# The modulation vector's groups on VectorE: spread over heads two to eight

## The chip, the core and the metric

The kernel runs on one core of a Trainium2 chip. The core has a matrix engine (TensorE), three engines for elementwise work (VectorE, ScalarE, GpSimd), and SyncE, whose queue issues the DMAs. The metric is the device time of one execution in microseconds, as the median of several runs. All engines run side by side and wait for each other on semaphores.

## The reference, cut to what matters

One inference step of a one-layer backbone on 2048 latent tokens and 128 context tokens, with 1024 channels:

```
mod   = split(silu(c) @ ada_w + ada_b, 6)      # for latents, and the same with c_ctx for context
h     = rms_norm(x, norm_mix_w) * (1 + mod[1]) + mod[0]
y     = hgrn2_mixer(h)                         # 8 heads: projections, two scans in chunks, gate, w_out
x     = x + mod[2] * y
h     = rms_norm(x, norm_ffn_w) * (1 + mod[4]) + mod[3]
x     = x + mod[5] * conv_ffn(h)
y_out = rms_norm(x, final_norm_w)
```

The modulation vector `mod` has 6 x 1024 numbers for the latents and as many for the context. The kernel holds it as 48 columns of 128 numbers, eight columns for each of the six parts. Parts 0 and 1 are needed before the first head. Parts 2 to 5, columns 16 to 47, are needed only after the eight heads: part 2 when the mixer's output is added to the residual, the others in the feed-forward part.

## The kernel before, in words

**Stages.** The tokens are cut into pieces of 512 (four of latents) and one of 128 (context). After a start that computes the first columns of `mod` and the first norm, a loop goes over the eight heads. For each head and each piece it projects the normed tokens to a query, two forget gates, a value and an output gate (matmuls of lines 416 to 418 and 538 to 540), and runs the chunkwise scan. Then comes the output projection (`project`, line 950), the second norm, and the feed-forward part in two stages (lines 1076 and 1307), which together take up more than the second half of the time.

**The scan's steps.** A head has eight steps, two for each latent piece; the context piece's projections come in the eighth. The scan of a head is cut into small units, and `scan_steps` (line 803) says into which step each goes, so that a unit runs while TensorE is at the projections of later pieces. The units of a head reach nine steps beyond its own eight, into the next head, and for head eight into the output projection. Three of them matter here. `unit1a` (line 577) is VectorE's work on decays, some forty instructions. `unit2` (line 673) multiplies keys and values on TensorE (line 692), copies a part on ScalarE (line 698) and updates the forward state on VectorE (lines 708 and 710). `unit3` (line 713) forms the output on TensorE and reads that state (line 730). So line 730 waits for line 708, and that for line 692.

**The groups.** Columns 16 to 47 are computed without TensorE. `ada_one(j)` (line 319) loads 128 rows of transposed weights (512 KB) through SyncE's queue into a buffer of the tag `wr`, and VectorE multiplies them by the broadcast conditioning vector and sums along the row, once for the latents and once for the context:

```
nc.sync.dma_start(raw, adaT[i * P : (i + 1) * P, :])
for s in range(2):
    junk = rt([P, D], F16, "og" if tag == "wr" else "SB")
    V.scalar_tensor_tensor(junk, raw, 1.0, cs[s], ALU.mult, ALU.mult,
                           accum_out=mod[:, j, s : s + 1])
```

These two instructions are called a group here, and one of them a half. There are 32 groups, and the loop over heads calls one at the end of each step from the second head on (lines 910 to 912) until column 48 is reached: with eight steps in a head that is heads two to five. Behind the loop, small VectorE instructions add the bias (`ada_add`, line 282) and form the factors `wmod` (line 332) and `g64` (line 917). The two broadcast vectors `cs`, 4 KB in each partition each, are kept until the last group.

**Other loads.** `load_w` (line 405) loads the weights of the next head in the eighth step, in buffers of the same tag `wr`, and splits them on ScalarE and VectorE (line 413); behind the loop it does so with the output weights (`load_wo`, line 945).

**What sets the order.** The text of the program sets the order only in part. The tile framework puts the instructions of each engine in an order of its own, by the program's order as priority and by when it holds their inputs to be ready; each engine then takes its queue strictly in that order. SyncE's queue, with all DMA issues, is such a queue too. The places of the buffers in on-chip memory are planned by the kernel itself (`place`, line 109): it runs the program once with stand-ins that note at which operation each buffer is born and last used, and lays them out so that addresses are reused late.

Of the kernel before, what the change touches and what calls it, by code (L numbers as in the profile page):

```python
# [170 lines left out]
def backbone_kernel(ctx: ExitStack, tc: tile.TileContext, **io):  # L171
# [16 lines left out]
    def no_probe(shape, *_):  # L188
        return Probe(0, 0)

    stages(Counts(clock), probe, no_probe, no_probe, **io)
    for t in keep:
        t.last = NEVER
# [15 lines left out]
    def drt(shape, dt, tag):  # L209
        return dr.tile(shape, dt, tag=tag, name=tag)  # L210

    stages(nc, tl, pt, drt, **io)


def stages(nc, tl, pt, drt, xT, adaH, adaT, pvec, w_in, w_out, w_up, w_down, state, yT, st_out):
# [103 lines left out]
    def ada_one(j, tag="wr"):  # L319

        raw = rt([P, D], F32, tag)
        i = j - 4 if j < 8 else j - 12
# [5 lines that stand above are left out]
# [52 lines left out]
    def tick():  # L380

        for g in list(norms):
            if next(g, 0) == 0:
                norms.remove(g)
# [39 lines left out]
    def load_x(p):  # L424
        t0, n = PIECES[p]
        XS[p] = []
        if p == CTX:
            xc = rt([P, KT, n], F32, "wr")
            get = lambda k: xc[:, k]
        else:  # L430
            get = eight(("even", "odd", "lv", "lv")[p], [P, 512], F32)
        for k in range(KT):
            x = get(k)
            nc.sync.dma_start(x[:, :n], xT[k * P : (k + 1) * P, t0 : t0 + n])
            XS[p].append(x)
# [16 lines left out]
    def norm1(p, eng):  # L452
        begin(norm(XS[p], PIECES[p][1], SQ3, "o16", eng, lambda bc: norm1_out(p, bc)))
# [33 lines left out]
    def head_weights(hd):  # L487
        for i in range(3):
            head_qf(hd, i)
        head_vg(hd)  # L490
# [24 lines left out]
    def project_qf(hd, p, i):  # L515

        pj = pt([P, 512], "pj")
        qf_mm(hd, p, i, pj, range(KT))
        qf_out(hd, p, i, pj)

    def project_vg(hd, p):

        n = PIECES[p][1]
        nb = n // P
        hp = H[p]
        small = n != 512
        wvg = WT[hd][1]
        st = PC[hd, p]
        vt = tl([P, n], F32, "vc") if small else rt([P, 512], F32, "v")
        sg = tl([P, n], F32, "sgc") if small else rt([P, 512], F32, "sg")  # L530
        for j0 in range(0, nb, 2):
            m = min(2, nb - j0)
            pj = pt([P, 2, 2, P], "pj")
            for jj in range(m):
                tok = slice((j0 + jj) * P, (j0 + jj + 1) * P)
                o = pj[:, :, jj, :]
                for k in range(KT):
                    T.matmul(o, hp[k][:, 0, tok], wvg[0][:, k], start=(k == 0), stop=False)  # L538
                    T.matmul(o, hp[k][:, 0, tok], wvg[1][:, k], start=False, stop=False)  # L539
                    T.matmul(o, hp[k][:, 1, tok], wvg[0][:, k], start=False, stop=(k == KT - 1))  # L540
            A.activation(vt[:, j0 * P : (j0 + m) * P].rearrange("p (b c) -> p b c", c=P),
                         pj[:, 0, :m], AF.Copy, scale=IWS)
            A.activation(sg[:, j0 * P : (j0 + m) * P].rearrange("p (b c) -> p b c", c=P),
                         pj[:, 1, :m], AF.Silu, scale=IWS)
        st["v"] = vt
        st["sg"] = sg
# [293 lines left out]
    def run(items):  # L840
        for f, *args in items:
            f(*args)
# [39 lines left out]
    nada = [16]  # L882

    for hd in range(HEADS):
        for p in range(CTX):
            for part in range(2):
                i = hd * NSEG + 2 * p + part
                run(before[i])
                if i < 2:
                    tick()  # L890
                else:
                    project_qf(hd, p, 2 * part)
                    tick()
                run(mid.get(i, []))
                if part == 1:
                    project_vg(hd, p)
                elif i > 0:
                    project_qf(hd, p, 1)
                if (p, part) == (3, 1):
                    for i3 in range(3):  # L900
                        project_qf(hd, CTX, i3)
                    project_vg(hd, CTX)
                    if hd + 1 < HEADS:
                        head_weights(hd + 1)
                run(after[i])
                if i in (1, 3, 5):
                    if i == 3:
                        load_x(3)
                    norm1((i + 3) // 2, V)
                if hd > 0 and nada[0] < 48:  # L910
                    ada_one(nada[0])
                    nada[0] += 1
    ada_add(16, 48, mod[:, 16:48])
# [562 lines left out]
```

## Time and profile before

| | |
|---|---|
| median of 3 runs | 2772.4 us (2771.98 to 2774.57) |
| the profiled execution | 2777.14 us, its span 2775.2 us |
| TensorE matmul / weight loads busy | 2705.4 / 2129.1 us |
| VectorE busy | 1886.0 us |
| ScalarE busy | 1071.8 us |
| DMA, mean rate | 86 GB/s |
| the 64 instructions of the groups | 182.6 us (first start) to 758.3 us (last start) |

The span runs from the first to the last instruction of the profiled execution. Busy time is the time in which an engine has at least one instruction of compute under way. Line numbers (L326) are those of the kernel, and tile names are those of the program. A group's row gives busy time and mean duration, then the idle time of the engine ahead of it and what ended it. A row of a timeline begins with start and duration in microseconds; a wait stands in brackets with the instruction that ended it. A row of stretches begins with the stretch and its length, then for each engine the busy time and, in brackets, the number of instructions; at the end stand the granted TensorE clock as a share of full speed, the DMA share and the rate.

The heads in this profile, from the start of a head's first projection: head two at 179.8 us, three at 325.7, four at 470.2, five at 614.1, six at 757.9, seven at 901.8, eight at 1045.6; head eight's projections end at 1190.2 us.

### The profile page before, as it was taken

Reading aid. Unit: us, or ns where it says so; the run is one execution under the profiler, and the core shown is the slowest. Engines: PE = TensorE matmul, PEld = TensorE weight load, DVE = VectorE, ACT = ScalarE, POOL = GpSimd, SP = SyncE. Lnnn points to the kernel's source line nnn. Section 1 sums busy time; section 2 is a strip of 40 time slices with the busy share of each in tenths; the row PEclk is TensorE's granted clock in tenths of the full one; section 3 lists DMA queues with packets and bytes.
Section 4 is the critical chain, followed back from the end, with each engine's and each line's share of the span. In section 5 each row is a group of like instructions: output and inputs, shape, how many; then the busy total and the mean of one; then the engine's idle time right before and its main releaser. Section 6 shows DMA issues by size and latency. Waiting matters only on the chain.

```text
span 2775.2 us, 57195 instructions
## 1 busy us (share of the span) xinstructions
PE 2705.4 (97%) x23576; PEld 2129.1 (77%) x23576; DVE 1886.0 (68%) x5324; ACT 1071.8 (39%) x2373; POOL 72.9 (3%) x84
## 2 busy tenths in 40 slices
PE   8999999999999999999999999999999999999998
PEld 4677777777777677765578888888888988888887
DVE  7887887887876766755996767666677677623123
ACT  5533334343434242513664545445455453300000
POOL 0100000000000000000000000000000000000000
PEclk9999999999999999999999999999999999999999
DMA  7011213121201010345112232221212275344352
GB/s 265 27 63 42 70 34 95 32 74 39 73 6 54 6 54 4 110 137 194 67 41 85 63 89 67 73 86 56 86 58 77 77 200 170 127 156 137 123 166 73
DMA packets 194005, 239.73 MB, mean 86 GB/s; under 512 B 12368, under 2 KB 148432, under 8 KB 193744
## 3 DMA queue, kind: packets, MB, share of 16 engines
q1 hardware_dynamic: 193744, 236.08, 26.9%
q8 instruction: 185, 3.03, 0.5%
q14 instruction: 76, 0.62, 0.1%
HBM read 166.44 MB, written 69.60 MB: 85 GB/s over the span
## 4 chain that ended last, share of the span: by engine, by line
PE 58%; DVE 16%; DMA 5%; ACT 2%; issue 2%; POOL 0%; SPq 0%; DVEq 0%; POOLq 0%; ACTq 0%
PE pj_p L1307 11%; PE pj_p L1076 9%; PE sc_p L1076 6%; PE pj_p L418 5%; PE pj_p L416 5%; PE pj_p L417 5%; DMA r<-w_up 3%; PE pj_p L539 3%; PE pj_p L538 3%; PE pj_p L540 3%; DMA ud<-u 2%; DVE u L971 2%; PE sc_p L1307 1%; PE sc_p L692 1%; DVE wd L1233 1%
## 5 line engine op out<-in xcount | busy, mean ns | idle before, releaser
L1076 PEld LDWEIGHTS <-w 128*128 128x128 f16 x7392 | 725.0, 98 | 115.4 <-issue 29.7
L1076 PE MATMUL pj_p<-T,w 128*128 128x256 f16 x4224 | 491.0, 274 | 24.2 <-DVE c L1082 16.4
L1307 PEld LDWEIGHTS <-wd 128*128 128x128 f16 x3696 | 361.5, 98 | 53.5 <-issue 8.8
L1076 PE MATMUL sc_p<-T,w 128*128 128x256 f16 x3168 | 367.8, 273 | 0.0
L1307 PE MATMUL pj_p<-U,wd 128*128 128x256 f16 x3168 | 354.3, 273 | 5.7 <-DVE x L1316 5.7
L416 PE MATMUL pj_p<-H,wp 128*128 128x512 f16 x768 | 291.2, 380 | 2.8 <-ACT H L395 2.4
L417 PE MATMUL pj_p<-H,wp 128*128 128x512 f16 x768 | 292.6, 381 | 0.5 <-DVE H L400 0.4
L418 PE MATMUL pj_p<-H,wp 128*128 128x512 f16 x768 | 292.3, 381 | 0.0
L540 PE MATMUL pj_p<-wp,H 128*128 128x256 f16 x1024 | 279.1, 273 | 0.0
L538 PE MATMUL pj_p<-wp,H 128*128 128x256 f16 x1024 | 279.1, 273 | 0.0
L539 PE MATMUL pj_p<-wp,H 128*128 128x256 f16 x1024 | 279.1, 273 | 0.0
L1316 DVE SCALAR_TENSOR_TENSOR x<-pj_p,g,x 128x256 f32<-128x256 f32 x96 | 46.4, 483 | 211.6 <-PE pj_p L1307 211.5
L418 PEld LDWEIGHTS <-wp 128*128 128x128 f16 x960 | 94.2, 98 | 91.4 <-issue 2.6
L416 PEld LDWEIGHTS <-wp 128*128 128x128 f16 x960 | 94.3, 98 | 83.5 <-issue 4.2
L417 PEld LDWEIGHTS <-wp 128*128 128x128 f16 x960 | 94.2, 98 | 81.1 <-issue 2.0
L363 ACT ACTIVATE n<-x 128x256 f32<-128x256 f32 (+1 forms) x63 | 25.0, 403 | 262.9 <-DVE x L1316 201.9
L1103 ACT ACTIVATE y<-c,pv,cws 128x512 f32<-128x512 f32 x88 | 71.2, 811 | 137.1 <-DVE c L1082 133.9
L511 ACT ACTIVATE f<-pj_p 128x512 f32<-128x512 f32 x64 | 38.0, 596 | 185.2 <-PE pj_p L418 185.1
L539 PEld LDWEIGHTS <-H 128*128 128x128 f16 x1024 | 100.2, 98 | 11.8
L540 PEld LDWEIGHTS <-H 128*128 128x128 f16 x1024 | 100.2, 98 | 11.7
L538 PEld LDWEIGHTS <-H 128*128 128x128 f16 x1024 | 100.3, 98 | 11.5
L417 PE MATMUL pj_p<-og,wo 128*128 128x512 f16 (+1 forms) x320 | 108.9, 349 | 0.0
(281 smaller groups left out, 5037.6 us busy)
## 6 DMA issues: line engine op xcount, KB each, us to landing
ud<-u SPq DMA_DIRECT2D x44, 896.0 KB, 4.8
U<-ud SPq DMA_DIRECT2D x56, 704.0 KB, 4.9
r<-w_up SPq DMA_DIRECT2D x44, 512.0 KB, 4.0
wr<-w_in SPq DMA_DIRECT2D x40, 512.0 KB, 4.2
wr<-adaT SPq DMA_DIRECT2D x32, 512.0 KB, 3.7
rawd<-w_down SPq DMA_DIRECT2D x20, 704.0 KB, 8.1
x<-xT SPq DMA_DIRECT2D x32, 256.0 KB, 5.3
sp<-oT SPq DMA_DIRECT2D x32, 256.0 KB, 2.2
```

The source lines that it names most:

```text
L416: T.matmul(out, whl[0], hhl[:, 0, :n], start=first, stop=False)
L417: T.matmul(out, whl[0], hhl[:, 1, :n], start=False, stop=False)
L418: T.matmul(out, whl[1], hhl[:, 0, :n], start=False, stop=last)
L511: A.activation(ft, pj[:, :n], AF.Tanh, scale=0.5 * IWS)
L538: T.matmul(o, hp[k][:, 0, tok], wvg[0][:, k], start=(k == 0), stop=False)
L539: T.matmul(o, hp[k][:, 0, tok], wvg[1][:, k], start=False, stop=False)
L540: T.matmul(o, hp[k][:, 1, tok], wvg[0][:, k], start=False, stop=(k == KT - 1))
L971: V.tensor_tensor(dst[1], src, dst[0], ALU.subtract)
L1076: T.matmul(out, wt[:, a, ks], tt[:, b, k], start=first and k == 0 and n == 0, stop=i in (2, 3, 4) and k == 3 and n == 2, skip_group_check= ...
L1103: A.activation(y, a, AF.Identity, bias=pv[:, PV_CB + cb : PV_CB + cb + 1], scale=cws[:, 22 + cb : 23 + cb])
L1307: T.matmul(out, w[:, a, k], UT[p, zb][b][:, k], start=first and i % 2 == 0 and k == 0 and q == 0, stop=n in (2, 3, 4) and k == KP - 1 and ...
L1316: V.scalar_tensor_tensor(x, get(src), g64[:, 1, m, 0:1], x, ALU.mult, ALU.add)
```

## The change

One condition is added. A group is now called only in steps whose number `i` (counted through all heads, eight to a head, from 0) gives `4 * i % 7` below 4, that is in four of every seven steps:

```diff
-                if hd > 0 and nada[0] < 48:
+                if hd > 0 and nada[0] < 48 and 4 * i % 7 < 4:
                     ada_one(nada[0])
                     nada[0] += 1
     ada_add(16, 48, mod[:, 16:48])
```

`i` runs from 8 to 63 in heads two to eight; 32 of these 56 numbers fulfil the condition, so all 32 groups are still called inside the loop, the last one in step 63, the eighth of head eight. The instructions of a group, its load and its tags are the same as before. With the calls, the births and last uses of the buffers move, those of `cs` among them, and so the plan of the places is drawn anew.

## The prediction

> **What bounds the kernel now.** I read the page first, for which engine fills the span, and then went to the part that the change touches: the scan over heads two to eight.
>
> ```profile
> span 2775.2 us, 57195 instructions
> ...
> PE 2705.4 (97%) x23576; PEld 2129.1 (77%) x23576; DVE 1886.0 (68%) x5324; ACT 1071.8 (39%) x2373; POOL 72.9 (3%) x84
> ```
>
> TensorE is busy for 97% of the span, VectorE for 68%. The average mixes stages, so the second view is the busy time by head. I cut the span where TensorE begins the projections of a head; heads two to five hold all 32 groups, heads six to eight none.
>
> ```profile
> core 0: us, PE busy (x) PEld busy (x) DVE busy (x) ACT busy (x) POOL busy (x), PEclk, DMA share, GB/s
> ...
> 179.80:325.70 145.90, 144.04 (x1206) 103.95 (x1204) 116.16 (x443) 51.77 (x136) 5.33 (x5) 1.00 0.18 53
> 325.70:470.20 144.50, 143.97 (x1208) 104.05 (x1206) 117.16 (x454) 51.83 (x137) 5.24 (x5) 1.00 0.19 58
> 470.20:614.10 143.90, 143.90 (x1208) 103.92 (x1206) 119.02 (x458) 52.37 (x137) 4.83 (x5) 1.00 0.18 58
> 614.10:757.90 143.80, 143.80 (x1207) 104.02 (x1206) 116.92 (x448) 52.14 (x137) 4.79 (x5) 1.00 0.19 58
> 757.90:901.80 143.90, 143.90 (x1208) 103.94 (x1206) 103.82 (x446) 52.14 (x137) 5.09 (x5) 1.00 0.10 29
> 901.80:1045.60 143.80, 143.80 (x1207) 103.97 (x1206) 99.99 (x426) 52.05 (x137) 5.36 (x5) 1.00 0.09 29
> 1045.60:1190.20 144.60, 144.19 (x1210) 104.20 (x1208) 106.30 (x437) 55.88 (x141) 4.71 (x5) 1.00 0.22 66
> ```
>
> This table carries most of the argument. The first number after each stretch is its length. Heads four and five carry the groups and take 143.9 and 143.8 us; heads six and seven carry none and take 143.9 and 143.8 us. VectorE is busy for 119.0 and 116.9 us in the first pair and for 103.8 and 100.0 us in the second, and the length doesn't notice: TensorE has no gap in any of the four. Only heads two (145.9), three (144.5) and eight (144.6) are longer, by 2.1, 0.7 and 0.8 us over 143.8.
>
> The third view says what TensorE waited for from head two until just behind head eight. Its columns are the total, the number of times and the longest.
>
> ```profile
> PE sc_p L730 <- DVE SF L708: 4.4, 2, 3.1
> PE sc_p L661 <- ACT oT L769: 1.1, 2, 0.6
> PE sc_p L692 <- ACT kT L670: 0.4, 1, 0.4
> ```
>
> Over 1,023 us that is 5.9 us of waiting, of which VectorE causes 4.4 us in two waits, both at the same place: the output matmul of line 730 wants the forward state that line 708 writes. So the whole prize within these heads is small, and the question is what the change does to these two waits.
>
> **The change part by part.** The groups themselves are moved, not removed.
>
> ```profile
> L326 DVE SCALAR_TENSOR_TENSOR og<-wr,wp 128x1024 f16<-128x1024 f32 x64 | 76.3, 1217 | 1.7 <-DMA wr<-adaT 1.6
> ```
>
> The 64 instructions take 76.3 us, so a group of two takes 2.4 us and one of its halves 1.2 us. By the new rule (step number times four, modulo seven, below four) heads two to eight get 4, 5, 4, 5, 4, 5 and 5 groups, 32 in all, the last in the last step of head eight. VectorE thus loses 4, 3, 4 and 3 groups in heads two to five (9.5 or 7.2 us each) and gains 4, 5 and 5 in heads six to eight (9.5, 11.9, 11.9 us). As heads four to seven show, neither matters to the length of a head that is filled by TensorE: 0 us, covered by VectorE's free time, at least 24 us in a head (143.9 less 119.0), and after the change at least that in heads two to seven.
>
> The first wait is in head two, and the groups cause it. These are VectorE's rows and TensorE's rows around it, start and duration first.
>
> ```profile
> 198.98 1.22 DVE L326 SCALAR_TENSOR_TENSOR og<-wr,wp 128x1024 f16<-128x1024 f32 x1
> ...
> 200.13 0.34 DVE L708 SCALAR_TENSOR_TENSOR SF<-SF,D128f,sc_p 128x128 f32<-128x128 f32 x1
> ```
>
> ```profile
> 192.36 1.05 PE L692 MATMUL sc_p<-v,kT 128*128 128x128 f32 x8
> ...
> 200.53 0.49 PE L730 MATMUL sc_p<-SF,q 128*128 128x128 f32 x2 [1.26 <-DVE SF L708]
> ```
>
> Line 708 could have started when line 692 ended, at 193.4 us; it started 6.7 us later, behind queued work with a group's second half right in front of it. The first step of head two now has no group, and the wait is 1.26 us, about one half. I take the wait as gone: -1.3 us (0 to -1.3). The two waits on line 769 (1.1 us) are between ScalarE and TensorE; I leave them, 0 (0 to -1.1).
>
> The second wait is at the end of head eight, where the change adds work.
>
> ```profile
> 1189.10 1.06 PE L692 MATMUL sc_p<-v,kT 128*128 128x128 f32 x8
> ...
> 1194.37 0.80 PE L730 MATMUL sc_p<-SF,q 128*128 128x128 f32 x2 [3.12 <-DVE SF L708]
> ```
>
> ```profile
> 1193.99 0.33 DVE L708 SCALAR_TENSOR_TENSOR SF<-SF,D128f,sc_p 128x128 f32<-128x128 f32 x1
> ```
>
> ```profile
> 1194.37:1197.78 3.41, 3.41 (x28) 2.58 (x29) 2.30 (x10) 0.93 (x3) 0.00 (x0) 0.50 0.35 121
> 1197.78:1200.66 2.88, 2.88 (x9) 1.14 (x8) 2.42 (x11) 0.00 (x0) 0.00 (x0) 0.51 0.00 0
> ```
>
> Line 708 starts 3.8 us after line 692 ended (1190.16), and TensorE waits 3.12 us. Behind the wait the granted clock is 0.50 and 0.51 for 3.41 and 2.88 us, so half of 6.3 us, 3.1 us, is lost on top. The place costs 6.2 us now. The wait of 1.26 us in head two cost no clock (its row above has 1.00), so between 1.3 and 3.1 us lies a cliff.
>
> [...]
>
> How much group work comes in front of line 708? VectorE's busy time just before it:
>
> ```profile
> 1144.80:1155.80 11.00, 2.03 (x5) 1.00 0.43 138
> 1155.80:1194.40 38.60, 36.84 (x146) 0.99 0.55 171
> ```
>
> From 1144.8 to 1155.8 us VectorE is free for 9.0 us; then it is full (36.8 of 38.6 us) until the wait. Head eight's groups are in its first, third, fifth, seventh and eighth steps. The earlier ones meet the free 9.0 us, enough for three groups (7.2 us). The last falls in the full stretch. Where it will stand is best read from head five, whose last step also has a group.
>
> ```profile
> 758.35 1.18 DVE L326 SCALAR_TENSOR_TENSOR og<-wr,wp 128x1024 f16<-128x1024 f32 x1
> ...
> 759.66 0.34 DVE L708 SCALAR_TENSOR_TENSOR SF<-SF,D128f,sc_p 128x128 f32<-128x128 f32 x1
> ```
>
> ```profile
> 756.87 1.06 PE L692 MATMUL sc_p<-v,kT 128*128 128x128 f32 x8
> ...
> 763.33 0.39 PE L730 MATMUL sc_p<-SF,q 128*128 128x128 f32 x2
> ```
>
> There a half ran between the end of line 692 (757.93) and line 708. In head five this cost nothing, because 5.4 us of projections lay before line 730; in head eight there are none, as the next head's are missing. I take one half in front: +1.2 us. The bounds are -6.2 (the place vanishes) and +7.1 us (three whole groups in front, no free time used).
>
> SyncE's queue is in order, and each group brings one issue into it. In heads six and seven it is moved past the states, spills and weights; in head eight it also stands ahead of the loads of the output weights.
>
> ```profile
> SPq L407 <- DVE og L326: 35.0, 3, 15.1
> ```
>
> ```profile
> 1180.16 1.28 DVE L413 SCALAR_TENSOR_TENSOR wo<-wr,gw,wo 128x1024 f16<-128x1024 f32 x1
> ```
>
> ```profile
> 1197.05 0.63 PE L416 MATMUL pj_p<-og,wo 128*128 128x512 f16 x1
> ```
>
> Now a weight load already waits up to 15.1 us for a group to free its buffer. The last output weight is split by 1181.4 us, and the first matmul on these weights starts at 1197.05: 15.6 us of cover, just over that. I take 0; if the cover is gone, each us of delay beyond it is a us of TensorE. ScalarE and GpSimd get no instruction.
>
> The additions behind the loop (lines 282, 332 and 917) now wait for the last group, about head eight's end. What is queued behind them is the residual of line 959, and TensorE waits for it only when all four accumulators of that tag are full. 0 us.
>
> Last, buffers are laid out by a planner that knows the order of all operations, so addresses shift, and with them waits, also later. TensorE's longest wait behind 1203 us is this:
>
> ```profile
> PE pj_p L418 <- DVE wd L1233: 3.7, 1, 3.7
> ```
>
> I put 0, with 3.7 us either way. **The sum**: -1.3 + 1.2 = -0.1 us on the span of 2775.2 us. That profiled execution took 2777.14 us in all, 1.9 us more than its span and 4.7 us above the median of 2772.4 us; the difference carries over to the median: 2772.3 us. A measurement of this kernel can tell about 0.2%, 5.5 us, from no change.
>
> **The rivals.** *The end gap closes.* The order on the engines isn't the program's but that of a scheduler that goes by when it thinks work is ready. With VectorE fuller it may put the first output projection ahead of line 730, as the projections in head five are. Then 6.2 us go at the end and 1.3 us in head two: 2772.4 - 7.5 = 2764.9 us. For it: the loop's next matmuls (1197.05) are there to fill the wait. Against it: nothing in the change asks for it. Chance 0.17.
>
> *VectorE's queue at the end.* The mechanism is line 708 behind group work in head eight. If the free 9.0 us don't serve, because the earlier steps' groups slip past them, three groups stand in front: +7.1 us, -1.3 us in head two, 2778.2 us; with the 3.7 us of shifted buffers, more. It decides from three groups on: 5.5 + 1.3 = 6.8 us. For it: the stretch is full and its wait is already there. Against it: in head five, with eight groups, line 708 was 1.7 us late, not 3.8. Chance 0.13.
>
> *The groups don't go where the text puts them.* A weight load that the program writes behind head eight was issued in the middle of it:
>
> ```profile
> 1113.73 0.33 SPq L407 DMA_DIRECT2D wr<-w_out  x1
> ```
>
> If groups are drawn ahead likewise, the end stays as it is and only the 1.3 us of head two go: 2771.1 us. Chance 0.10.
>
> **How the numbers follow.** The forecast, TensorE still filling the heads and the two waits moving against each other, has the remaining 0.60 and gives 2772.3 us. With the third rival it makes no measurable change: 0.70. Faster is the first rival, 0.17; slower the second, 0.13. The range runs from 2763.8 us (the first rival's 2764.9 less the 1.1 us of the waits on line 769) to 2780 us (the second's 2778.2 and half of the 3.7 us of shifted buffers, 1.8); what is left out is more than one mishap at a time.
>
> **What would show it.** Heads three to seven should be 143.8 to 144.5 us long with VectorE at about 107 to 116 us in each. The wait in head two should be gone. At the end of head eight the wait before line 730 should be between 3 and 6 us, with a clock of 0.5 behind it, and a half of the last group shortly before line 708. I am wrong on the end if that wait is absent or over 9 us; wrong on the base if heads six and seven grow by more than 1 us with waits on line 708; and wrong on the rest if the time behind 1203 us differs by over 4 us.

## The result, and the profile after

The changed kernel takes 2790.27 us (median of 4 runs, 2785.37 to 2791.56); the kernel before, run beside it, 2773.49 us (4 runs, 2771.98 to 2776.08). The ratio is 1.0056 (95% interval 1.0044 to 1.0069): slower by 0.56%, above the forecast's range of 2763.8 to 2780 us. The profiled execution took 2791.56 us, its span 2789.9 us.

The first lines of the profile's page, of the changed kernel:

```profile
span 2789.9 us, 57218 instructions
...
PE 2712.0 (97%) x23576; PEld 2132.7 (76%) x23576; DVE 1885.1 (68%) x5324; ACT 1071.8 (38%) x2373; POOL 70.5 (3%) x84
```

The span grew by 14.7 us, and TensorE's busy time, with as many matmuls, by 6.6 us. So some matmuls ran slower and the rest is waiting. The table by head, cut at the same matmuls as before, shows that it isn't the heads:

```profile
178.60:322.40 143.80, 143.80 (x1206) 103.92 (x1204) 106.28 (x425) 51.61 (x136) 4.91 (x5) 1.00 0.13 42
322.40:466.20 143.80, 143.80 (x1207) 103.97 (x1206) 107.18 (x440) 51.68 (x137) 5.10 (x5) 1.00 0.15 47
466.20:610.10 143.90, 143.90 (x1208) 104.00 (x1206) 109.38 (x432) 51.88 (x137) 4.99 (x5) 1.00 0.14 44
610.10:753.90 143.80, 143.80 (x1207) 103.95 (x1206) 105.85 (x425) 52.22 (x137) 4.82 (x5) 1.00 0.15 47
753.90:897.80 143.90, 143.90 (x1208) 104.01 (x1206) 112.68 (x456) 52.43 (x137) 5.10 (x5) 1.00 0.13 44
897.80:1041.80 144.00, 143.91 (x1207) 103.94 (x1206) 107.01 (x430) 51.93 (x137) 4.74 (x5) 1.00 0.15 47
1041.80:1186.30 144.50, 144.03 (x1210) 104.14 (x1208) 117.73 (x454) 55.87 (x141) 5.05 (x5) 1.00 0.25 81
```

All seven heads are 143.8 to 144.5 us long; head two became shorter by 2.1 us and head three by 0.7. VectorE's load is level, as the change meant. If one compares the start of each matmul in both traces, the changed kernel is 1.2 us ahead where head two begins, 4.0 us ahead where head eight's projections end, 0.9 us ahead at 1203 us, and 14.4 us behind from 2434 us to the end. So the end of head eight cost 3.0 us and the output projection and feed-forward part 15.3 us. Of these, about 1.7 us fall between 1203 and 1420 us (times of the kernel before), 3.7 us between 1420 and 2200 us, and 10.0 us behind that.

The end of head eight first: TensorE, VectorE and the stretches there (start and duration, a wait in brackets).

```profile
1185.13 1.06 PE L692 MATMUL sc_p<-v,kT 128*128 128x128 f32 x8
...
1192.18 0.69 PE L652 MATMUL sc_p<-qh,kh 128*64 128x64 f32 x6 [5.16 <-DVE qh L624]
1193.85 0.80 PE L730 MATMUL sc_p<-SF,q 128*128 128x128 f32 x2 [0.99 <-DVE SF L708]
```

```profile
1175.00 1.23 DVE L326 SCALAR_TENSOR_TENSOR og<-wr,wp 128x1024 f16<-128x1024 f32 x1 [2.20 <-DMA sp<-oT]
...
1181.04 1.22 DVE L326 SCALAR_TENSOR_TENSOR og<-wr,wp 128x1024 f16<-128x1024 f32 x1
...
1193.45 0.34 DVE L708 SCALAR_TENSOR_TENSOR SF<-SF,D128f,sc_p 128x128 f32<-128x128 f32 x1
```

```profile
1192.20:1199.40 7.20, 6.21 (x36) 3.83 (x37) 6.28 (x34) 0.93 (x3) 0.00 (x0) 0.50 0.31 95
```

TensorE now waits 5.16 and 0.99 us in place of 3.12 us. The longer wait is for line 624, which comes ahead of line 708 in VectorE's queue. Line 708 starts 7.3 us after line 692 ended (1186.19), where it was 3.8 us. The last half runs at 1181.04 us, 12 us ahead of line 708; ahead of the one at 1175.00 us VectorE stood idle for 2.20 us, because the place of its scratch output `og` was still being read by a store of `oT`. The two halves and this wait come to 4.65 us. How much of line 708's delay they make can't be read here, since the order of VectorE's other instructions changed too; the last experiment prices the groups at this place.

Then the stretch from 1203 us, before and after, between the same matmuls:

```profile
1203.00:2420.00 1217.00, 1179.32 (x10858) 989.48 (x10857) 857.04 (x1543) 583.19 (x1165) 15.56 (x11) 0.99 0.31 95
```

```profile
1202.10:2434.40 1232.30, 1187.00 (x10858) 993.15 (x10857) 860.00 (x1556) 583.77 (x1165) 13.88 (x11) 0.99 0.31 94
```

The stretch grew by 15.3 us: TensorE's gaps (length less busy time) from 37.7 to 45.3 us, 7.6 us, and its busy time, for the same 10,858 records, by 7.7 us. Nearly all of the latter is the clock: its records show 30.7 us at half clock against 17.1 us, and half of the 13.6 us between them is 6.8 us. TensorE's waits there, of the changed kernel:

```profile
PE pj_p L1076 <- DVE c L1082: 16.6, 12, 3.1
PE sc_p L1076 <- ACT c L1091: 6.1, 1, 6.1
PE pj_p L1076 <- ACT c L1085: 5.9, 10, 1.7
PE pj_p L418 <- DVE wd L1233: 5.1, 2, 3.0
```

In the kernel before the same kinds of wait were:

```profile
PE pj_p L1076 <- DVE c L1082: 16.4, 14, 2.6
PE pj_p L1076 <- ACT c L1089: 4.1, 2, 2.9
PE pj_p L418 <- DVE wd L1233: 3.7, 1, 3.7
...
PE pj_p L1076 <- ACT c L1085: 2.4, 6, 0.6
```

The instructions are the same; what differs is above all who waits for whom, and for how long. The longest, 6.13 us at 2286.68 us, can be followed back. SyncE, VectorE, ScalarE and TensorE of the changed kernel:

```profile
2260.52 18.28 SPq L1228 DMA_DIRECT2D rawd<-w_down  x7
2278.85 3.01 SPq L1191 DMA_DIRECT2D uc<-u  x2
```

```profile
2284.93 0.42 DVE L1147 TENSOR_TENSOR t<-y 128x256 f32<-128x256 f32 x1 [11.70 <-DMA uc<-u]
```

```profile
2285.73 0.63 ACT L970 ACTIVATE u<-t 128x512 f16<-128x512 f32 x1 [9.99 <-DVE t L1148]
2286.27 0.37 ACT L1091 ACTIVATE c<-sc_p 128x256 f32<-128x256 f32 x1
```

```profile
2286.68 3.65 PE L1076 MATMUL sc_p<-T,w 128*128 128x256 f16 x15 [6.13 <-ACT c L1091]
```

Seven loads of `w_down` take 18.28 us to be issued, since most of them wait for their places: SyncE has five waits of 1.3 to 3.0 us among them, and the shortest issue takes 0.37 us. Behind them stands the store of `u`. VectorE wants to write `t` where that store still reads, and waits 11.70 us; ScalarE's copy of `t` waits for VectorE, and behind it in ScalarE's queue stands line 1091, which frees the accumulator that TensorE wants. The `t` of this gate has nothing to do with the stored `u`, and line 1091 nothing with `t`: a shared address ties the first pair, the order of ScalarE's queue the second.

### The profile page after: what moved, and what is told of

The parts are those of the page before. It is cut to its first block, busy times and chain, and to the rows that moved or that the text cites. A ratio compares the mean times of both kernels' runs of the same rounds, so it can differ in the third digit from the quotient of the medians.

```text
span 2789.9 us, 57218 instructions
## 1 busy us (share of the span) xinstructions
PE 2712.0 (97%) x23576; PEld 2132.7 (76%) x23576; DVE 1885.1 (68%) x5324; ACT 1071.8 (38%) x2373; POOL 70.5 (3%) x84
## 4 chain that ended last, share of the span: by engine, by line
PE 73%; DVE 15%; DMA 6%; ACT 3%; issue 2%; SPq 0%; POOL 0%; DVEq 0%; POOLq 0%; ACTq 0%
PE pj_p L1307 10%; PE pj_p L1076 10%; PE pj_p L418 7%; PE pj_p L417 7%; PE pj_p L416 7%; PE sc_p L1076 7%; PE pj_p L540 4%; PE pj_p L539 4%; PE pj_p L538 4%; DMA r<-w_up 3%; DMA ud<-u 2%; PE sc_p L692 2%; PE sc_p L1307 1%; PE sc_p L652 1%; DVE u L971 1%
## 5 line engine op out<-in xcount | busy, mean ns | idle before, releaser
L1076 PE MATMUL pj_p<-T,w 128*128 128x256 f16 x4224 | 492.2, 274 | 24.4 <-DVE c L1082 16.6
```

The source lines that it names most:

```text
L1076: T.matmul(out, wt[:, a, ks], tt[:, b, k], start=first and k == 0 and n == 0, stop=i in (2, 3, 4) and k == 3 and n == 2, skip_group_check= ...
```

## The experiments

The theory at this point: the plan of the places, drawn anew, costs the time (**places**). The rival: the groups' calls in the new steps cost it, or shift the order for all that follows (**calls**). In each run the kernel before ran beside it; times are compared by the ratio to that (medians of the kernel before 2774.3 to 2776.8 us).

**Calls and places crossed.** Two kernels. The first has the new calls, and for all buffers born behind the loop the places of the kernel before; the heads' buffers keep the changed kernel's places, except where they live into the last 200 operations of the loop. The second is the mirror: old calls, later buffers at the changed kernel's places.

```diff
-    at = next(a for a in (place(tiles, far) for far in (600, 300, 200, 100, 50, 20)) if a)
+    _, at0, k0 = plan(OTHER, {})
+    tiles, at1, _ = plan(OWN, {})
...
+    fixed.update((i, at0[i]) for i in late)
+    tiles, at, _ = plan(OWN, fixed)
...
-                if hd > 0 and nada[0] < 48:
+                if hd > 0 and nada[0] < 48 and RULE[0](i):
```

> The changed calls of the groups, but every buffer born behind the loop over heads at its place of the kernel before; buffers of the heads at their places of the changed kernel, except the last 200 operations. The trace of the changed kernel is 1.0 us ahead of the kernel before at 1250 us and 14.4 us behind from 2400 us on. Places theory (the 15 us behind the heads come from the redrawn places of the feed-forward buffers): 2772.5 us, between 2769 and 2776. Calls theory (they come from VectorE's later groups, whatever the places): 2790 us, between 2785 and 2793. Chance theory (the later stage differs from drawing to drawing of the clock alone): anything between 2770 and 2790, and apart from run to run.

> The mirror image: the calls of the kernel before (every step of heads two to five), but every buffer born behind the loop at its place of the changed kernel. Places theory: the kernel before plus the 15.4 us, 2789 us, between 2785 and 2792, with VectorE's line 1147 waiting for the store of line 1191 as in the changed kernel. Calls theory: 2773.5 us, between 2771 and 2776.

Measured: new calls at the old later places 2767.99 us, ratio 0.9976 (0.9966 to 0.9986); old calls at the new later places 2793.2 us, ratio 1.0067 (1.0054 to 1.0079). Each lies a little outside the range of the places theory (2769 to 2776 and 2785 to 2792 us), on the side away from the calls theory. The slowness goes with the places: 0.9% lies between the two plans. The calls theory falls. In the second kernel TensorE waits 7.4 us at 2286 us where the changed kernel waits 6.1. In the first the end of head eight holds only 1.4, 0.6 and 0.5 us of waits, with the same groups in the same steps, so there too the buffers' places, not the group alone, decide.

**Two more draws of the kernel before.** One puts groups in two of three steps, which ends them in head seven; the other only changes the planner's first limit.

```diff
-                if hd > 0 and nada[0] < 48:
+                if hd > 0 and nada[0] < 48 and i % 3 < 2:
```

```diff
-    at = next(a for a in (place(tiles, far) for far in (600, 300, 200, 100, 50, 20)) if a)
+    at = next(a for a in (place(tiles, far) for far in (900, 300, 200, 100, 50, 20)) if a)
```

> The groups in two of every three steps of heads two to seven, none in head eight, places drawn anew by the kernel's own planner. Both theories: the 4.0 us that the changed kernel has gained by 450 us stay gained at 1200 us, where it loses 3.0 of them to the last group. Places theory: what follows depends on the drawing; as the order on the engines behind the heads is that of the kernel before, 2769.5 us, between 2766 and 2774. Calls theory (any spreading costs later): 2785 us or more.

> The kernel before with one number of its planner of places changed (the first limit on the distance between two uses of an address, 900 operations in place of 600); calls and computation as before. Places theory: a redraw alone moves the time by several us, by 4 to 20 either way, most of it behind 1300 us. Calls theory: within 2.5 us of the kernel before, 2771 to 2776.

Measured: 2774.01 us, ratio 0.9994 (0.9984 to 1.0003), and 2779.42 us, ratio 1.0020 (1.0010 to 1.0029). The first was expected at 2766 to 2774 us. The groups in heads two to seven make no difference that can be told; a wait of 2.7 us stays at the end of head eight without any group there. The second shows that a new draw alone, with not one operation changed, moves the time.

**One place, one queue, one group, one more draw.** Four edits of the changed kernel:

```diff
-    at = next(a for a in (place(tiles, far) for far in (600, 300, 200, 100, 50, 20)) if a)
+    at = next(a for a in (place(tiles, far) for far in (600, 300, 200, 100, 50, 20)) if a); at[2948] = 209920
```

```diff
-        nc.sync.dma_start(UC[:, cb], u)
+        nc.scalar.dma_start(UC[:, cb], u)
```

```diff
+OWN = lambda i: (4 * i % 7 < 4 and i < 63) or i == 61
...
-                if hd > 0 and nada[0] < 48:
+                if hd > 0 and nada[0] < 48 and RULE[0](i):
```

The third is printed against the kernel before, cut to the rule of the calls; it also pins all buffers but the groups' own to the changed kernel's places. The fourth sets the planner's first limit to 900, as above.

> Theory (a reused place in the feed-forward stage): in the changed kernel one 2 KB buffer, the buffer t written at L1147 in the last gate, lies where 26 to 58 operations earlier the store of u still reads; that store stands behind seven loads of w_down in SyncE's queue, and VectorE waits 11.70 us, TensorE 6.13 us behind it at 2286 us. This kernel moves that one buffer and nothing else; the order of TensorE's 40954 rows stays. Expected: VectorE's wait at L1147 under 1 us, TensorE's wait at 2286 under 2 us, half clock there 3.4 us or none: 6 to 9 us less than the changed kernel, 2780 to 2784 us. Rival (the late store only finds another victim, as the weight split was in the kernel before): a wait of 2.9 us or more stands elsewhere behind the same store, gain 0 to 3 us, 2787 to 2790 us. Rival (the calls or the whole plan, not this place): no gain, 2789 to 2791 us.

> The 22 stores of u in the feed-forward stage (L1191) are issued by ScalarE instead of SyncE, same plan as the changed kernel. Theory (the store is late because it stands in SyncE's queue behind the loads of w_down, whose issue waits 18.28 us for buffers): the store starts when its data are there, the wait of 11.70 us at L1147 falls under 3 us and TensorE's 6.13 us at 2286 with it: 6 to 9 us less there; 22 issues on ScalarE, off the path, cost 0 to 2 us in all: 2780 to 2786 us. Rival (the store is late because its data are late, or its transfer is slow): the wait stays over 8 us, 2789 to 2792 us. Rival (ScalarE's issues hold back the sums at L1085 and L1089 that TensorE waits for): more waits on ScalarE, over 2792 us.

> The changed calls with the last of the 32 groups in step 61 of 64 instead of step 63; the buffers of everything else stay at the changed kernel's places. Theory (the group that ran into the end of head eight holds back the operations there): TensorE's waits at 1192 us fall from 5.16 and 0.99 us to 3.1 us or less in sum, half clock from 10.2 to 6.8 us or less: 2 to 4 us less than the changed kernel, 2786.5 to 2788.5 us. Rival (where the buffers of the last head lie decides): waits there of 5 to 6 us as in the changed kernel, 2789.5 to 2791.5 us. By both the feed-forward stage loses its 14 to 16 us as in the changed kernel.

> The changed kernel with the planner's first limit at 900 operations instead of 600, which draws another plan. Theory (what the change costs is one unlucky plan, the calls themselves gain 0.24 percent): the heads still end 3 to 5 us ahead of the kernel before; the feed-forward stage costs what its own draw gives, between what was seen of four draws (5 us less to 15 us more): 2765 to 2787 us, and less than the changed kernel's 2790.3. Rival (plans for the new calls are bad as a class): 2787 to 2793 us. The theory gives no closer number, as a draw can't be worked out from the traces.

*One buffer moved*: 2789.15 us, ratio 1.0047 (1.0035 to 1.0059), and the rival of the next victim is right. The wait at line 1147 is gone, and this stands in its place (what waited, in the stretch from 2255 to 2300 us):

```profile
ACT wd L1232 <- DMA uc<-u: 8.8, 1, 8.8
```

A weight split wants a place that the same late store holds; TensorE's 6.1 us became 5.7.

*The store from ScalarE*: 2786.9 us, ratio 1.0038 (1.0025 to 1.0052), just above the theory's range, and TensorE's wait stays. VectorE's fell from 11.7 to 3.0 us, about as expected, but ScalarE's weight splits now wait 3.3 us for `uc` and 7.3 us for `ud`, the larger stores that are still in SyncE's queue, and TensorE waits 5.6 us at 2281 us. Taking one line out of the queue frees little.

*The last group two steps earlier*: 2789.69 us, ratio 1.0045 (1.0030 to 1.0060). The waits at 1195 us fell to 1.9 and 1.2 us, the theory's 3.1, but an earlier one took their place. ScalarE, and TensorE's longest wait from 1140 to 1203 us (this kernel's lines stand 27 lower down the file):

```profile
1154.48 1.15 ACT L439 ACTIVATE wo<-wr,gw 128x1024 f16<-128x1024 f32 x1 [9.26 <-DMA wr<-w_out]
```

```profile
PE sc_p L688 <- ACT oT L796: 4.0, 1, 4.0
```

A half ran at 1147.16 us, and the next load of an output weight was issued at 1148.42 us, when that half had ended; ScalarE, in order, waited 9.26 us for it, and TensorE 4.0 us for ScalarE. This is the SyncE term that the prediction put at 0 under 15.6 us of cover. The cover that it meant still stands here: the last weight is split by 1185.3 us and its first matmul starts at 1199.47. The delay reached TensorE on another path, through `oT`, which stands behind the weight split in ScalarE's queue.

*Another draw for the new calls*: 2782.01 us, ratio 1.0021 (1.0011 to 1.0032), between the ends that the theory gave and far from a fixed cost of the calls.

**All stores of the gates from GpSimd**, in the changed kernel, the kernel before, and the fastest so far:

```diff
-        nc.sync.dma_start(UD[p][:, :, :, cb // 2], u)
+        nc.gpsimd.dma_start(UD[p][:, :, :, cb // 2], u)
...
-        nc.sync.dma_start(UC[:, cb], u)
+        nc.gpsimd.dma_start(UC[:, cb], u)
```

> The changed kernel with the 42 or so stores of u in the feed-forward stage (L1158 and L1191) issued by GpSimd, which has nothing to do there, instead of SyncE; same plan, same calls. Theory (the places act through SyncE's queue: the loads of w_up and w_down stand behind stores that wait for a gate, and stores stand behind loads that wait for their place, so that VectorE and ScalarE wait for both): VectorE's 11.7 us at L1147 and TensorE's 6.13 us at 2286 fall under 2 us each, the waits of VectorE and ScalarE for r from w_up (36.5 and 64.5 us) fall by at least a third, TensorE's waits on L1082 from 16.6 to under 12 us, and of the 15.4 us lost behind 1203 us at least 9 come back: 2774 to 2782 us. Rival (the places act through the order of work on the engines, not through the queue): 2788 to 2792 us. Rival (GpSimd issues its stores later than SyncE did): waits on uc and ud grow, over 2792 us.

> The same edit on the kernel before. Theory of the queue: the kernel before has the same two kinds of wait in smaller sizes (ScalarE 6.0 us for uc at 2274, TensorE 2.92 us), so it gains less: 2767 to 2774 us, and the difference of 17 us between the changed kernel and this one shrinks to under 9 us once neither has the stores in SyncE's queue. Rival (order of work): 2772 to 2777 us, difference 13 to 18 us.

> The same edit on the changed calls with the later buffers at the places of the kernel before (2767.99 us, 0.24 percent under the kernel before). Theory of the queue: as with the kernel before, 1 to 8 us less, 2760 to 2767 us, the fastest version. Rival: no gain, 2766 to 2770 us.

Measured: 2810.88 us (ratio 1.0129, 1.0109 to 1.0149), 2808.82 us (1.0123, 1.0106 to 1.0141) and 2801.52 us (1.0096, 1.0080 to 1.0111). The theory of the queue fails in all three: each is some 20 to 34 us slower than without the edit. What SyncE's loads waited for, and the issues from 1420 to 2300 us (KB each, median us from the start of the issue to landing), in the first of the three:

```profile
SPq L1043 <- DMA ud<-u: 557.4, 15, 66.7
```

```profile
ud<-u POOLq DMA_DIRECT2D x41, 896.0 KB, 5.4
```

where the changed kernel has

```profile
ud<-u SPq DMA_DIRECT2D x42, 896.0 KB, 4.8
```

With no store ahead of them the loads of `w_up` were at the head of the queue, and 15 of them still waited for a store of `u` to land: for the place it reads, not for the queue. From the start of its issue a store landed after 4.8 us from SyncE and 5.4 us from GpSimd; the issue, which is part of that, took 0.52 and 1.05 us, so 0.5 of the 0.6 us lie in the longer issue. From SyncE it also started sooner behind the last instruction of line 971, which writes `u`: 0.03 us behind its end in the median, against 0.30 us from GpSimd. So a store released its place some 0.9 us later, 37 us over the 41 stores if every one bound; 20 to 34 us fit that. It isn't shown: VectorE's and ScalarE's waits for `w_up`, which this account would lengthen, come to 100 us in the first of the three and to 102 us in the changed kernel. The difference between changed kernel and kernel before shrank to 2 us.

**The place of `w_up`'s loads.** So the planner is told that each buffer `r` (line 1043) is needed 200 operations before its load, and its place is then free for at least 210 operations; in the changed kernel's plan 20 of the 44 loads have only 89 to 121. The same for the kernel before; a third kernel lets the planner hold each `u` for 60 operations longer; the fourth, a control, only sets the limit to 200, with which the first ends up too.

```diff
-        tiles.append(Probe(clock[0], nbytes(shape, dt)))
+        tiles.append(Probe(clock[0] - (200 if tag == "r" else 0), nbytes(shape, dt)))
```

```diff
-        tiles.append(Probe(clock[0], nbytes(shape, dt)))
+        tiles.append(Probe(clock[0], nbytes(shape, dt))); tiles[-1].late = 60 if tag == "u" else 0
...
-    stages(Counts(clock), probe, no_probe, no_probe, **io)
+    stages(Counts(clock), probe, no_probe, no_probe, **io); [setattr(t, "last", t.last + t.late) for t in tiles]
```

> The changed kernel; the planner counts each buffer r, into which w_up is loaded (L1043), as needed 200 operations before its load is issued, so that its place has been free for at least 210 operations by then (in the changed kernel 20 of 44 loads had 89 to 121). Theory (the loads of w_up wait in SyncE's queue for a place that a late store or operation of a gate still holds, and VectorE and ScalarE then wait for w_up): VectorE's and ScalarE's waits for r from w_up in 1420 to 2300 us fall from 36.5 and 64.5 us to under half, TensorE's waits on L1082 from 16.6 to under 8 us, and 6 to 12 us come back behind 1400 us: 2776 to 2785 us, if the rest of the plan is drawn no worse. Rival (other places take over, since memory is full): waits move to other buffers, 2787 to 2795 us.

> The same rule for r in the kernel before. Theory: the waits for w_up fall to under half, TensorE's waits on L1082 there (some 13 us) to under 6 us: 2762 to 2770 us, faster than the kernel before. Rival (other places take over): 2772 to 2785 us.

> The changed kernel; the planner counts each buffer u as held for 60 operations more, so that no load of w_down (rawd, L1228) finds a place that a store of u issued one to three operations before. Theory (the stores of u in SyncE's queue and the loads of w_down hold each other up at 2260 to 2290 us): TensorE's wait of 6.13 us at 2286 falls under 3 us and the distance to the kernel before grows by under 2 us between 2250 and 2320 us instead of 4 us; the rest is another draw, 2770 to 2792 us. Rival: a wait of 5 us or more stays there.

> A control for the first: the changed kernel with the planner's first limit at 200 operations, which the first kernel ends up with too, and without its rule for r; 21 of 44 loads of w_up have 29 to 120 operations' distance. By the theory of w_up's places waits for r of the changed kernel's size stay (30 to 40 and 55 to 75 us) and the time is 5 us or more over the first kernel's; by the rival (only the limit matters) both have the same time within 3 us.

Measured: changed kernel with the rule 2764.21 us, ratio 0.9956 (0.9943 to 0.9969), the fastest of all; kernel before with the rule 2768.98 us, 0.9976 (0.9966 to 0.9985); the control 2783.12 us, 1.0030 (1.0020 to 1.0041). The waits from 1420 to 2300 us, of the changed kernel:

```profile
SPq L1043 <- DMA ud<-u: 59.7, 14, 4.5
```

```profile
ACT w L1037 <- DMA r<-w_up: 64.5, 15, 7.5
DVE s L1048 <- DMA r<-w_up: 30.4, 8, 5.3
DVE s L1049 <- DMA r<-w_up: 6.1, 1, 6.1
```

and with the rule:

```profile
SPq L1043 <- DMA ud<-u: 14.2, 4, 5.0
```

```profile
DVE s L1048 <- DMA r<-w_up: 7.4, 3, 2.6
DVE s L1050 <- DMA r<-w_up: 6.9, 3, 3.3
ACT w L1037 <- DMA r<-w_up: 5.9, 2, 4.7
DVE s L1049 <- DMA r<-w_up: 2.6, 1, 2.6
...
PE pj_p L1076 <- DVE c L1082: 1.8, 4, 0.7
```

With places free in time the loads come early, ScalarE's and VectorE's waits for `w_up` fall from about 100 to 23 us, and TensorE's on line 1082 from 16.6 to 1.8 us, as the theory said; in the kernel before the two fall to 37 and 5.1 us. The whole time fell by 26 us under the changed kernel, where 6 to 12 us were expected. But the rule draws all other places anew too, so the stage itself has to be looked at. By the starts of the same matmuls in the profiled executions, against the kernel before (minus is faster; times of the kernel before):

| | waits for `w_up`, us | 1420 to 2200 us | 2200 us to the end |
|---|---|---|---|
| kernel before | 95 | 0 | 0 |
| changed kernel | 102 | +3.7 | +10.0 |
| control (limit 200) | 50 | -12.8 | +21.5 |
| kernel before, rule for `r` | 37 | -16.8 | +18.5 |
| changed kernel, rule for `r` | 23 | -18.4 | +15.6 |

The fewer the waits for `w_up`, the shorter the stage: the theory holds for it. Behind 2200 us the three redrawn plans lose most of that again, or more, and why wasn't followed; what the two kernels with the rule keep in the end comes mostly from ahead of 1420 us (9.0 and 6.2 us). The control had VectorE's waits of 37.2 us as expected, but ScalarE's of 13.3 us only, where 55 to 75 us were expected; so it is no clean control, and its 19 us over the first kernel aren't these loads alone.

*u held longer*: 2780.09 us, ratio 1.0017 (1.0008 to 1.0026). The wait of 6.1 us at 2286 us is gone, as expected; but from 2300 to 2400 us TensorE has this:

```profile
PE sc_p L368 <- DVE n L364: 15.5, 1, 15.5
```

Places seem to be short elsewhere instead; which one this wait goes back to wasn't followed.

**The calls alone.** Last, the groups in the steps of the kernel before, with all of the 3,088 other buffers at the changed kernel's places; only the calls, and the places of the groups' own 96 buffers, differ from the changed kernel.

> The calls alone: the groups in the steps of the kernel before, while every one of the 3088 other buffers, those of the heads too, stands at the changed kernel's place. Theory (the calls are worth nothing that can be told, all of the change's effect is the plan): 2787 to 2794 us, as the changed kernel, and the heads end 3 to 5 us ahead of the kernel before, as there. Rival (the calls themselves gain the 4 us of the heads): the heads end within 1.5 us of the kernel before, and the whole is 3 to 5 us over the changed kernel, 2793 to 2796 us. Rival (the calls themselves cost, at the end of head eight, where the changed kernel lost 3 us): that loss is gone, 2786 to 2788 us.

Measured: 2790.49 us, ratio 1.0060 (1.0047 to 1.0073), the changed kernel's time. At these places the calls as such are worth nothing that can be told in the whole time; the 0.56% goes with the plan. Within that, from the start of head two to the end of the heads the same matmuls gain 1.4 us on the kernel before here and 2.8 us in the changed kernel, so the calls gain about 1.4 us and the places as much. The heads end 2.9 us ahead of the kernel before, where the theory had 3 to 5.

Where they gain it is not where the prediction had it. From head two's start to 280 us the distance between the two kernels doesn't change: the wait of 1.26 us in head two is gone here too, with the groups in their old steps. VectorE and TensorE of this kernel (lines 27 lower down the file, so that 353, 735 and 757 are 326, 708 and 730):

```profile
194.53 1.22 DVE L353 SCALAR_TENSOR_TENSOR og<-wr,wp 128x1024 f16<-128x1024 f32 x1
...
195.67 0.34 DVE L735 SCALAR_TENSOR_TENSOR SF<-SF,D128f,sc_p 128x128 f32<-128x128 f32 x1
```

```profile
197.67 0.39 PE L757 MATMUL sc_p<-SF,q 128*128 128x128 f32 x2
```

A half still stands right in front of the state's update, and the output matmul doesn't wait. In the kernel before with another first limit, with its own calls, this wait is gone as well. The calls' 1.4 us lie further on, the larger part in head four, where this kernel's matmuls lose 1.0 us and the changed kernel's none.

At the end of head eight TensorE waits, in this kernel:

```profile
PE sc_p L679 <- DVE qh L651: 1.4, 1, 1.4
PE sc_p L757 <- DVE SF L735: 1.2, 1, 1.2
```

It gains 1.8 us there on the kernel before where the changed kernel loses 3.0: at these places head eight's groups cost 4.8 us. In these two profiles the feed-forward part gives some of it back (this kernel loses 17.9 us behind 1203 us, the changed one 15.3).

## Why the prediction was wrong

**Heads, 0 for the moved groups: right.** All seven heads are as long as TensorE's work. **Head two, -1.3 us: right in size, by luck.** The wait is gone as forecast, but it is also gone with the groups in their old steps, in the calls-alone kernel and in the kernel before with another first limit: the places were enough. Whether the moved calls would have ended it at the old places, no run shows. The calls' own 1.4 us came from later heads, where the step had put 0.

**End of head eight, +1.2 us: mis-sized.** It lost 3.0 us against the kernel before, and head eight's groups cost 4.8 us at equal places. The step counted one half, right in front of line 708, and that with its length alone. No run shows that a longer wait adds only its length: the granted clock was 0.50 there for 10.2 us from 1189.2 us on, against 6.8 us from 1193.8 us on in the kernel before. The step didn't count the group's other half, nor that a half can stand idle in VectorE's queue for its scratch output's place (2.20 us), with all behind it; and the longer of TensorE's two waits, 5.16 us, was not on line 708 but on line 624 ahead of it. Of the rivals, the second had the mechanism, VectorE's queue, with three groups and 7.1 us. The first and the third rival didn't happen: the waits are there, and the last halves run at 1175 and 1181 us.

**SyncE's queue, 0 under 15.6 us of cover: right where the change puts the groups.** With the last group two steps earlier, a load behind a half cost TensorE 4.0 us, through ScalarE's queue, a path that the step didn't have.

**"Buffers are laid out by a planner ... I put 0, with 3.7 us either way": this step failed.** The new places cost 15.3 us behind 1203 us, where the prediction had called itself wrong from 4 us on. The bound was one wait, the longest that the old plan left. But a plan decides not one wait but some forty loads and as many stores of a stage in which TensorE has 37.7 us of gaps, and some of the new waiting is paid again at half clock (some 7 of the 15.3 us). The trace of before had a warning: waits of 33.1 and 59.5 us of VectorE and ScalarE for `w_up` from 1420 to 2300 us, in a stage that another plan made 18 us shorter. They show how much hangs on places; they are nearly the same in the changed kernel and don't carry its loss.

What stays open: how the 15.3 us divide over single places. 10.0 us of them lie behind 2200 us, and the one wait there that I could follow to TensorE was replaced by its neighbour when its buffer was moved. No run has the new calls with the whole old plan, the heads' places included. Shown is that the plan carries the difference.

## What to carry to other kernels

Where a planner lays out full memory, an edit's cost is its own plus a draw of the plan: here the same or nearly the same operations took from 2764 to 2793 us by the places alone, and an edit worth 0.1% can't be read off one draw. Cross the edit with the plan (new calls with old places, and the reverse), before believing either sign. And look for loads that wait for a store to land: give these buffers a place that is free well ahead of the issue, with it the stage that loads `w_up` became 17 to 18 us shorter than in the kernel before. Then look at what the redraw took back: in the whole, the changed kernel went from 0.56% slower than the kernel before to 0.44% faster, and the kernel before gained 0.24%.

## What the runs showed of the hardware

The prediction put a cliff between waits of 1.3 and 3.1 us, below which the clock holds. The length of a wait alone doesn't place it. In the changed kernel the clock fell after one of 2.07 us, the smaller of the two waits on line 418, in a stretch in which TensorE was idle for 2.0 of 4.3 us:

```profile
2363.36 0.27 PE L418 MATMUL pj_p<-U,wd 128*128 128x128 f16 x1 [2.07 <-DVE wd L1233]
```

```profile
2359.00:2363.30 4.30, 2.29 (x42) 2.12 (x38) 4.30 (x5) 3.39 (x5) 0.00 (x0) 1.00 0.60 158
2363.40:2366.80 3.40, 3.40 (x33) 3.40 (x34) 2.69 (x6) 1.89 (x3) 0.00 (x0) 0.50 0.00 0
```

A longer wait of the same kernel, 2.78 us from 2037.3 us on, left the clock at full speed for the 10 us behind it:

```profile
2037.30:2050.00 12.70, 9.86 (x89) 8.70 (x89) 8.85 (x15) 5.48 (x11) 0.00 (x0) 1.00 0.01 1
```

The stretch behind the wait of 2.07 us is 3.40 us at 0.50, behind 2.0 us of idling. What the clock goes by, these runs don't show.
